# A read-back moved behind the attention projections, and adaLN weights loaded three steps ahead, in a two-layer diffusion step

## The chip, the cores and the metric

The kernel runs on one core of a Trainium2 chip. The core has five engines that run side by side, each with its own instruction stream: TensorE (PE, matrix products; its weight loads are shown as PEld), VectorE (DVE), ScalarE (ACT), GpSimd (POOL) and SyncE (SP), which here only issues DMA transfers. Sixteen DMA engines carry the transfers of the core. The metric is the device time of one launch in microseconds, the median over runs; smaller is better.

## What is computed

One inference step of a two-layer hybrid backbone over 128 context and 1024 latent tokens (a grid of 16 rows of 64), width 1024. Each layer is x + gate * mixer(rmsnorm(x) * (1 + scale) + shift), where shift, scale and gate come from a small adaLN product of the conditioning vector. Layer 0 mixes by a gated linear recurrence (4 heads, two directions) and a neighbourhood attention, layer 1 by a convolution and a second recurrence. The parts that matter here:

```python
def adaln(cond, w_mod, b_mod):
    m = (jax.nn.silu(cond) @ w_mod + b_mod)[:, None, :]
    return jnp.split(m, 3, axis=-1)

def even_mixer(h, w_in, w_out, lb, out_gain, rel_bias, s0, ctx_kv):
    q_a, z_f, z_b, v_a, g_a, q_b, k_b, v_b, g_b = jnp.split(h @ w_in, ...)
    o_a, s_fin = hgrn2_bidirectional(q_a, z_f, z_b, v_a, lb, s0)
    o_b = neighbourhood_attention(qh, kh, vh, ctx_kv[0], ctx_kv[1], rel_bias)
    y = concatenate([o_a * silu(g_a), o_b * silu(g_b)])
    return y @ w_out, s_fin, kh, vh

# in neighbourhood_attention: for each block of 16 columns a band of 32 key columns
    v_blk = lax.dynamic_slice_in_dim(v_grid, rs, kh, axis=2)[:, :, :, col_idx]
```

The attention gathers its values in column bands: four bands of 32 columns that start at 0, 8, 24 and 32.

## The kernel before

**Products and weights.** The tokens are cut into three chunks of 384. A projection's weights come in blocks of 512 KB (`wraw`), which ACT splits into a high part (`wh`) and POOL into the rest (`wl`, L186); each product is three matmuls of the parts (L316 to L318). A unit is one block of 128 features by one chunk: 24 matmuls of 128x384 (`unit_f`, L320), or 24 of 128x256 for the values (`unit_v`). Activations and splits by ACT are all recorded at L77.

**Order.** Every load (L56) and store (L59) goes through SP's one queue in the order of the program: a transfer that has to wait for its data or its buffer holds up all behind it. Twenty buffers of one shape ("slabs") are shared by weights raw and split (`wraw`, `wh`, `wl`), adaLN weights (`wm`), keys and queries (`kq`), value tiles (`vbt`) and value bands (`vband`). An agenda counts the units: `at(u, f)` puts a piece of work behind unit u, and `tick` (L350) runs what is due after each unit. There are eight semaphore lanes for DMAs, so a transfer also waits for the one eight before it.

**The stretch in question**, some 430 to 650 us into the span, follows the last head of the recurrence:
- 18 value units (`vb_unit`), in two blocks b of nine token tiles t. In the second, after every second tile, `band_copy` (L719) stores a finished `vbt` (512 KB, to the scratch tensor `vb_d`) and right behind it loads four pieces of 256 KB back into two `vband` tiles: the same values, cut to bands of 32 columns. These loads stand in SP's queue directly behind the store they read from. There are 4 stores and 16 such loads.
- 36 projection units (four feature blocks p; for each a key, a query and a gate weight, for each of these three chunks). `w_get(i, 0, 1)` loads the next weight one block ahead. Key and query units are evacuated into `kq` by ACT, gate units into `yT` by ACT and DVE (L365, `gate_evac`). Three PSUM buffers take turns.
- between the projection units the adaLN groups 1 and 2: 8 steps each, `mod_step(g, k)`, of 8 matmuls (L221) on two `wm` tiles of 512 KB; the step loads those of the next. After the eighth, a row is loaded (`bmrow`), DVE adds it (`modR`, L227), two `gate_d` stores put out the gates, and four transposes (L234) give the modulation. These stand in the same tick as the eighth step.

The attention itself, which reads `vband`, follows behind all 36 units.

Of the kernel before, what the change touches and what calls it, by code (L numbers as in the profile page):

```python
# [22 lines left out]
# columns of the packed small parameters (feature on the partition)  # L23
# [10 lines left out]
def trunk_kernel(ctx: ExitStack, tc: tile.TileContext, x, wm0, wm, bmr, wfe, wv, woe, wfo, woo, rgw, sm, st0,  # L34
# [34 lines left out]
    def act(out, in_, func, **kw):  # L69
        """An activation; those that need a table of their own stay between its load and the next one."""  # L70
# [12 lines left out]
    # ------------------------------------------------------------------ constants  # L83
# [39 lines left out]
    # decay floors: the first entry of the softmax over the two logits  # L123
# [12 lines left out]
    # log1p(exp(-|lam|)) + max(-lam, 0), as a series in z = e / (2 + e) <= 1/3  # L136
# [21 lines left out]
    # ------------------------------------------------------------------ weight stream  # L158
# [43 lines left out]
    # ------------------------------------------------------------------ adaLN rows  # L202
# [26 lines left out]

    def mod_feat(R, tag):  # L230
        """[128, j, g, 32] features on the partition, from row blocks at partitions 32 g."""
        pt = psum(tag)
        for j in range(4):
            PE.transpose(pt[:, j * 128:(j + 1) * 128], R[:, j * 128:(j + 1) * 128], ident)  # L234
        return pt.rearrange("p (j g c) -> p g j c", j=4, c=32)
# [14 lines left out]
    # ------------------------------------------------------------------ norm, modulation, split  # L250
    hT = {}

    def stats(xt, junk, cuts=(0, D)):
        """1 / sqrt(mean of squares + eps) of each row."""
# [34 lines left out]
    def to_hT2(l, c, ks, xn, tag):  # L289
        """Two blocks at once, each engine's steps together."""  # L290
# [18 lines left out]
    # ------------------------------------------------------------------ units of the projections  # L309
# [10 lines left out]
    def unit_f(i, c, tag=None):  # L320
        """Features of one block of 128 on the partition, one chunk of tokens."""
        ucount[0] += 1
        ps = psum(tag or ("o" if i >= IFO and ucount[0] % 4 == 0 else "mm"))
        o = ps[:, :CW]
        for k in range(8):
            mm_f(o, i, c, k)
        return o

    def unit_v(i, t):
        """Tokens on the partition, 256 features."""  # L330
# [29 lines left out]
    def gate_evac(key, o, twice=False):  # L360
        """o sigmoid(o); twice that by way of sigmoid(o) = (1 + tanh(o / 2)) / 2."""
# [22 lines left out]
    # ------------------------------------------------------------------ start  # L384
# [81 lines left out]
    # ------------------------------------------------------------------ layer 0, gated recurrence  # L466
# [17 lines left out]
    def ew1(h, d):  # L484
        """Log decays, their running sums in chunks of 64 and the sums' distances from each chunk's middle."""
# [61 lines left out]
    def att(h, d):  # L547
        """Scores in blocks of 64 keys and 64 queries; the two directions meet in the blocks on the diagonal."""
# [29 lines left out]
    def ew3(h, d):  # L578
        """The second chunk's queries as seen from the state before the tile; keys as the state after it sees them."""
# [18 lines left out]
    def kv(h, d, gi):  # L598
        """State before each latent tile; the state after the context."""
# [66 lines left out]
    # units from a head's projections to each of its steps  # L666
    STEP = [0, 1, 3, 4, 7, 9, 10, 11, 13, 15, 17, 20, 21, 21]

    def head(h, first=None):
# [16 lines left out]
        for n in range(4):          # q, z_f, z_b, g  # L686
# [15 lines left out]
    # ------------------------------------------------------------------ layer 0, attention projections  # L702
# [16 lines left out]
    def band_copy(Rg):  # L719
        src = vbt.pop(Rg)  # L720
        store(vb_d[2 * Rg:2 * Rg + 2].rearrange("t p f -> p t f"), src)
# [8 lines left out]
    for b in range(2):  # L730
        w_get(IVB + 2 * b + 1, 2, 1)
        for t in range(9):
            vb_unit(b, t)
            if t == 5:
                w_get(IVB + 2 * b + 1, 2, 2)
            if b == 1 and t in (2, 4, 6, 8):
                band_copy(t // 2 - 1)
# [4 lines left out]
    # adaLN, the other groups  # L742
    mst = {}

    def mod_step(g, k):
# [5 lines left out]
        if k < 7:  # L751
            mod_load(g, [k + 1])
        elif g == 1:
            mod_load(2, [0])
        if k == 7:
            R = mod_evac(g, mst["ps"], mod_row(g))
            if g == 1:
                gate_rows(0, R, 0)
                set_B(1, mod_feat(R, "b"), 2)
            else:  # L760
                set_A(1, mod_feat(R, "b"), 0)
                gate_rows(1, R, 2)
# [3 lines left out]
    def rows_of(c):  # L766
        """Grid rows of a chunk of tokens, cut at the middle row: (column in the chunk, first row, rows).
        A query tile holds its rows from the last to the first."""
# [138 lines left out]
    at(U + 2, mod_load, 1, [0])  # L907
    for g in (1, 2):
        for k in range(8):
            at(U + (4, 13)[g - 1] + k, mod_step, g, k)  # L910
    for p in range(4):
        for n in range(3):          # k, q, g
# [29 lines left out]
    # ------------------------------------------------------------------ layer 0, attention  # L942
# [15 lines left out]
    # ------------------------------------------------------------------ output projections  # L958
# [14 lines left out]
    def out_tiles(i0, ts, last=8, cuts=HALVES):  # L973
        """Row tiles of an output projection; the terms from last on come after those of all the tiles."""
# [14 lines left out]
    def resid(ps, gt, xt, cuts=HALVES):  # L989
        """xt += ps * gt; the product's tile is free afterwards."""  # L990
# [35 lines left out]
    # ------------------------------------------------------------------ layer 1  # L1026
# [13 lines left out]
    def xc_of(j, a, b):  # L1040
        """Tokens a to b of the convolution's result; the latents follow the context with a gap of 3."""
# [321 lines left out]
```

## Time and profile before

| | us |
|---|---|
| median of three runs | 1321.14 |
| the three runs | 1316.18, 1321.14, 1326.65 |
| span of the profiled execution | 1308.3 |
| PE busy | 1210.3 (93%) |
| PEld busy | 1076.2 (82%) |
| DVE busy | 692.2 (53%) |
| ACT busy | 540.4 (41%) |
| POOL busy | 380.4 (29%) |

The profiled execution's own time is not listed; only its span is. In the rows further down a timeline gives, for each group of equal instructions, the start, the duration, the engine and line, what it writes and reads, and in square brackets how long the engine was idle before it and what ended that wait. "SPq" is the queue of DMA issues on SP: its duration is the time until the last of them was issued, not until the data landed. [...]

### The profile page before, as it was taken

Reading aid. Unit: us, or ns where it says so; the run is one execution under the profiler, and the core shown is the slowest. Engines: PE = TensorE matmul, PEld = TensorE weight load, DVE = VectorE, ACT = ScalarE, POOL = GpSimd, SP = SyncE. Lnnn points to the kernel's source line nnn. Section 1 sums busy time; section 2 is a strip of 40 time slices with the busy share of each in tenths; the row PEclk is TensorE's granted clock in tenths of the full one; section 3 lists DMA queues with packets and bytes.
Section 4 is the critical chain, followed back from the end, with each engine's and each line's share of the span. In section 5 each row is a group of like instructions: output and inputs, shape, how many; then the busy total and the mean of one; then the engine's idle time right before and its main releaser. Section 6 shows DMA issues by size and latency. Waiting matters only on the chain.

```text
span 1308.3 us, 19176 instructions
## 1 busy us (share of the span) xinstructions
PE 1210.3 (93%) x7536; PEld 1076.2 (82%) x7536; DVE 692.2 (53%) x1422; ACT 540.4 (41%) x1065; POOL 380.4 (29%) x271
## 2 busy tenths in 40 slices
PE   4999999999999966999989999999989898988998
PEld 3889998999998964779966667888989798987886
DVE  5547128316365100000058897555568978799844
ACT  3435134334253201111136675323376676777311
POOL 0143023321414101111150420025445663645000
PEclk8999999999999997999979999999999989999999
DMA  9401000111101236562240215324001101112432
GB/s 353 179 33 37 17 19 23 53 33 37 33 23 43 95 120 208 173 209 75 65 158 13 95 66 177 113 81 145 17 25 41 41 25 41 41 33 81 145 129 81
DMA packets 41909, 110.45 MB, mean 84 GB/s; under 512 B 4180, under 2 KB 14804, under 8 KB 41820
## 3 DMA queue, kind: packets, MB, share of 16 engines
q1 hardware_dynamic: 41820, 109.24, 24.4%
q8 instruction: 59, 0.97, 0.3%
q14 instruction: 30, 0.25, 0.1%
HBM read 96.61 MB, written 12.61 MB: 83 GB/s over the span
## 4 chain that ended last, share of the span: by engine, by line
PE 36%; DVE 12%; ACT 6%; issue 4%; POOL 2%; DMA 1%; POOLq 0%; ACTq 0%; DVEq 0%; SPq 0%
PE ps_mm L316 5%; PE ps_mm L318 5%; PE ps_mm L317 5%; PE ps_mm L985 5%; PE ps_mm L984 4%; PE ps_mm L986 4%; DVE yT L1127 2%; DVE xc L1051 2%; DVE P L849 2%; ACT P L77 2%; ACT gr L77 1%; PE ps_a L221 1%; DMA bmrow<-in_bmr_dram 1%; DVE ps_mm L844 1%; ACT rt L77 1%
## 5 line engine op out<-in xcount | busy, mean ns | idle before, releaser
L316 PE MATMUL ps_mm<-hTh,wh 128*128 128x384 f32 x936 | 320.7, 347 | 9.9 <-ACT xp L77 4.8
L317 PE MATMUL ps_mm<-hTl,wh 128*128 128x384 f32 x936 | 319.8, 342 | 2.3 <-DVE hTl L307 1.7
L318 PE MATMUL ps_mm<-hTh,wl 128*128 128x384 f32 x936 | 319.4, 341 | 0.7 <-POOL wl L186 0.7
L186 POOL TENSOR_TENSOR wl<-wraw,wh 128x1024 fp32r<-128x1024 f32 x50 | 127.2, 2548 | 306.1 <-ACT wh L77 248.7
L316 PEld LDWEIGHTS ps_mm<-hTh,wh 128*128 128x128 f32 x936 | 177.8, 191 | 26.5 <-issue 6.5
L317 PEld LDWEIGHTS ps_mm<-hTl,wh 128*128 128x128 f32 x936 | 178.4, 191 | 4.8 <-DVE hTl L307 3.3
L318 PEld LDWEIGHTS ps_mm<-hTh,wl 128*128 128x128 f32 x936 | 178.2, 190 | 1.3 <-POOL wl L186 1.0
L985 PE MATMUL ps_mm<-wl,yh 128*128 128x512 f32 (+1 forms) x288 | 113.4, 394 | 4.6 <-DVE wl L186 4.5
L984 PE MATMUL ps_mm<-wh,yh 128*128 128x512 f32 (+1 forms) x288 | 112.7, 393 | 0.0
L986 PE MATMUL ps_mm<-wh,yl 128*128 128x512 f32 (+1 forms) x288 | 112.3, 390 | 0.0
L77 ACT ACTIVATE wh<-wraw 128x1024 fp32r<-128x1024 f32 x68 | 71.3, 1057 | 91.1 <-DMA wraw<-in_wfe_dram 67.3
L262 POOL TENSOR_TENSOR ss<-ss,nhalf 128x1 f32<-128x1 f32 x27 | 15.3, 565 | 242.9 <-DVE ss L261 185.8
L339 PE MATMUL ps_mm<-wh,hTh 128*128 128x256 f32 x288 | 82.6, 287 | 2.4 <-ACT va L77 2.4
L341 PE MATMUL ps_mm<-wh,hTl 128*128 128x256 f32 x288 | 81.2, 282 | 0.0
L340 PE MATMUL ps_mm<-wl,hTh 128*128 128x256 f32 x288 | 81.0, 281 | 0.0
L365 DVE SCALAR_TENSOR_TENSOR yT<-yT,ps_mm 128x384 f32<-128x384 f32 x10 | 5.5, 554 | 131.3 <-ACT yT L77 131.3
L77 ACT ACTIVATE res<-xt 128x512 f32<-128x512 f32 (+1 forms) x37 | 22.9, 619 | 123.3 <-DVE xt L994 115.5
L814 POOL TENSOR_TENSOR nbm<-mkt,bT 128x384 f32<-128x384 f32 x42 | 45.5, 1108 | 90.1 <-DVE nm L860 40.4
L985 PEld LDWEIGHTS ps_mm<-wl,yh 128*128 128x128 f32 x288 | 54.6, 189 | 19.0 <-DVE wl L186 7.7
L984 PEld LDWEIGHTS ps_mm<-wh,yh 128*128 128x128 f32 x288 | 54.5, 189 | 12.4 <-issue 0.3
L986 PEld LDWEIGHTS ps_mm<-wh,yl 128*128 128x128 f32 x288 | 54.4, 189 | 11.4
L1118 POOL TENSOR_TENSOR yT<-yT,rt 128x384 f32<-128x384 f32 x42 | 56.4, 1370 | 23.4 <-ACT rt L77 19.4
(260 smaller groups left out, 2477.3 us busy)
## 6 DMA issues: line engine op xcount, KB each, us to landing
wm<-in_wm_dram SPq DMA_DIRECT2D x48, 512.0 KB
wraw<-in_wfe_dram SPq DMA_DIRECT2D x28, 512.0 KB
xt<-in_x_dram SPq DMA_DIRECT2D x18, 512.0 KB
bT<-in_bias_dram SPq DMA_DIRECT2D x48, 192.0 KB
wraw<-in_wfo_dram SPq DMA_DIRECT2D x16, 512.0 KB
x_d<-xt SPq DMA_DIRECT2D x9, 512.0 KB
xt<-x_d SPq DMA_DIRECT2D x9, 512.0 KB
out_dram<-xt SPq DMA_DIRECT2D x18, 256.0 KB
```

The source lines that it names most:

```text
L77: i = A.activation(out, in_, func, **kw)
L186: (lo_eng or G).tensor_tensor(lo, r, hi.bitcast(F32), OP.subtract)
L316: PE.matmul(o, w1, hh, start=(k == 0), stop=False)
L317: PE.matmul(o, w1, hl, start=False, stop=False)
L318: PE.matmul(o, w2, hh, start=False, stop=(k == 7))
L339: PE.matmul(o, hh, w1, start=(k == 0), stop=False)
L340: PE.matmul(o, hh, w2, start=False, stop=False)
L341: PE.matmul(o, hl, w1, start=False, stop=(k == 7))
L984: PE.matmul(o[:, :q - p], yh[:, z], wh[:, p:q], start=(k == 0), stop=False)
L985: PE.matmul(o[:, :q - p], yh[:, z], wl[:, p:q], start=False, stop=False)
L986: PE.matmul(o[:, :q - p], yl[:, z], wh[:, p:q], start=False, stop=(k == 7))
L1118: G.tensor_tensor(us[c], us[c], r[:, c * CW:(c + 1) * CW], OP.mult)
```

## The change

Four things change, all in the stretch above; the computation is the same, and the rest of the diff takes comments out, which moves line numbers by up to nine.
- `band_copy` becomes `band_store`, in the same place, and `band_load`, put on the agenda at units U+20, U+23, U+26 and U+29 (U is the count at the start of the 36 projection units).
- The first three steps' `wm` loads (six of 512 KB) are issued in the second value block, ahead of tiles 2, 5 and 8.
- The 16 adaLN steps follow one another without a pause, at U+4 to U+19 (before: U+4 to U+11 and U+13 to U+20), and each loads the tiles of the step three further on.
- `mod_done` takes gate stores and transposes out of the eighth step to the next tick.

```diff
-    def band_copy(Rg):
-        src = vbt.pop(Rg)
-        store(vb_d[2 * Rg:2 * Rg + 2].rearrange("t p f -> p t f"), src)
+    def band_store(Rg):
+        store(vb_d[2 * Rg:2 * Rg + 2].rearrange("t p f -> p t f"), vbt.pop(Rg))
+
+    def band_load(Rg):
         v0 = vb_d[2 * Rg]
         for jp in range(2):
             t = slab("vband", (128, 2, 512))
...
         for t in range(9):
+            if b == 1 and t in (2, 5, 8):
+                mod_load(1, [t // 3])
             vb_unit(b, t)
             if t == 5:
                 w_get(IVB + 2 * b + 1, 2, 2)
             if b == 1 and t in (2, 4, 6, 8):
-                band_copy(t // 2 - 1)
+                band_store(t // 2 - 1)
...
-    def mod_step(g, k):
+    MODS = [(g, k) for g in (1, 2) for k in range(8)]
+
+    def mod_step(n):
+        g, k = MODS[n]
         if k == 0:
             mst["ps"] = psum("a")
         mod_mm(g, mst["ps"], [k])
         rows.pop((g, k, 0))
         rows.pop((g, k, 1))
-        if k < 7:
-            mod_load(g, [k + 1])
-        elif g == 1:
-            mod_load(2, [0])
+        if n + 3 < len(MODS):
+            mod_load(MODS[n + 3][0], [MODS[n + 3][1]])
         if k == 7:
-            R = mod_evac(g, mst["ps"], mod_row(g))
-            if g == 1:
-                gate_rows(0, R, 0)
-                set_B(1, mod_feat(R, "b"), 2)
-            else:
-                set_A(1, mod_feat(R, "b"), 0)
-                gate_rows(1, R, 2)
+            mst[g] = mod_evac(g, mst["ps"], mod_row(g))
+
+    def mod_done(g):
+        R = mst.pop(g)
+        if g == 1:
+            gate_rows(0, R, 0)
+            set_B(1, mod_feat(R, "b"), 2)
+        else:
+            set_A(1, mod_feat(R, "b"), 0)
+            gate_rows(1, R, 2)
...
     U = clock["u"]
-    at(U + 2, mod_load, 1, [0])
-    for g in (1, 2):
-        for k in range(8):
-            at(U + (4, 13)[g - 1] + k, mod_step, g, k)
+    for n in range(16):
+        at(U + 4 + n, mod_step, n)
+        if n % 8 == 7:
+            at(U + 4 + n + 1, mod_done, MODS[n][0])
+    for Rg in range(4):
+        at(U + 20 + 3 * Rg, band_load, Rg)
```

The order of SP's queue around the second value block was this; `fin` are final states and `vbc` the context's values, both stored to the output:

```order
L59 DMA out_dram<-vbc 128x512
L59 DMA out_dram<-fin 128x128 x2
L59 DMA vb_d<-vbt 128x2x512
L56 DMA vband<-vb_d 128x1x512 x4
L59 DMA vb_d<-vbt 128x2x512
L56 DMA vband<-vb_d 128x1x512 x4
L59 DMA vb_d<-vbt 128x2x512
L56 DMA vband<-vb_d 128x1x512 x4
L59 DMA vb_d<-vbt 128x2x512
L56 DMA vband<-vb_d 128x1x512 x4
L56 DMA wm<-in_wm_dram 128x1024 x2
L59 DMA out_dram<-kq 128x128
```

Of the change, the same place:

```order
L59 DMA out_dram<-vbc 128x512
L56 DMA wm<-in_wm_dram 128x1024 x2
L59 DMA out_dram<-fin 128x128 x2
L59 DMA vb_d<-vbt 128x2x512
L56 DMA wm<-in_wm_dram 128x1024 x2
L59 DMA vb_d<-vbt 128x2x512
L56 DMA wm<-in_wm_dram 128x1024
L59 DMA vb_d<-vbt 128x2x512
L56 DMA wm<-in_wm_dram 128x1024
L59 DMA vb_d<-vbt 128x2x512
L56 DMA wraw<-in_wfe_dram 128x1024
L59 DMA out_dram<-kq 128x128
```

The 16 reads of `vb_d` are gone from between the stores, and six `wm` loads stand there in their place, ahead of the projections.

On the same queue, the end of the projections, before, where the last `wm` loads and the last projection weights (`wraw`) are issued:

```order
L56 DMA wraw<-in_wfe_dram 128x1024
L56 DMA wm<-in_wm_dram 128x1024 x3
L59 DMA out_dram<-kq 128x128
L56 DMA wm<-in_wm_dram 128x1024
L56 DMA bmrow<-in_bmr_dram 128x1x512
L56 DMA wraw<-in_wfe_dram 128x1024
L59 DMA gate_d<-modR 2x512 x2
L56 DMA wraw<-in_wfe_dram 128x1024 x3
L59 DMA out_dram<-kq 128x128
```

And of the change:

```order
L59 DMA out_dram<-kq 128x128
L56 DMA vband<-vb_d 128x1x512
L59 DMA gate_d<-modR 2x512 x2
L56 DMA vband<-vb_d 128x1x512 x3
L56 DMA wraw<-in_wfe_dram 128x1024
L56 DMA vband<-vb_d 128x1x512 x4
L56 DMA wraw<-in_wfe_dram 128x1024
L56 DMA vband<-vb_d 128x1x512 x4
L56 DMA wraw<-in_wfe_dram 128x1024
L56 DMA vband<-vb_d 128x1x512 x4
L59 DMA out_dram<-kq 128x128
L56 DMA wraw<-in_wfe_dram 128x1024
```

The last four projection weights (those of gate block 2, key block 3, query block 3 and gate block 3) now each have reads of `vb_d` ahead of them, three or four at a time, and the second read stands behind the two `gate_d` stores.

On ACT, from the last evacuation of query block 2 on, before (a `yT` is an evacuation of a gate unit, a `kq` one of a key or query unit, a `wh` the split of a weight):

```order
L77 ACTIVATE kq<-ps_mm 128x6x4x16
L77 ACTIVATE wh<-wraw 128x1024
L77 ACTIVATE yT<-ps_mm 128x384 x3
L77 ACTIVATE kq<-ps_mm 128x384 x2
L77 ACTIVATE wh<-wraw 128x1024
L77 ACTIVATE kq<-ps_mm 128x384
```

And of the change:

```order
L77 ACTIVATE kq<-ps_mm 128x6x4x16
L77 ACTIVATE yT<-ps_mm 128x384
L77 ACTIVATE wh<-wraw 128x1024
L77 ACTIVATE yT<-ps_mm 128x384 x2
L77 ACTIVATE kq<-ps_mm 128x384 x2
L77 ACTIVATE wh<-wraw 128x1024
L77 ACTIVATE kq<-ps_mm 128x384
```

The split of the weight for query block 3 moved from ahead of the three `yT` to between the first and the second of them.

## Rows read from the trace of the kernel before

**Rows 1.** The page, first lines: span, and busy time of PE.
```profile
span 1308.3 us, 19176 instructions
...
PE 1210.3 (93%) x7536; PEld 1076.2 (82%) x7536; DVE 692.2 (53%) x1422; ACT 540.4 (41%) x1065; POOL 380.4 (29%) x271
```
**Rows 2.** Waits, 430 to 660 us: us in total, times, longest.
```profile
ACT wh L77 <- DMA wraw<-in_wfe_dram: 57.8, 7, 36.3
...
PE ps_a L221 <- DMA wm<-in_wm_dram: 20.3, 1, 20.3
...
POOL wl L186 <- DMA vb_d<-vbt: 8.6, 1, 8.6
...
PE ps_b L234 <- DVE modR L227: 2.3, 2, 1.8
```
**Rows 3.** PE's timeline, 453 to 516 us: start, duration.
```profile
455.45 0.46 PE L627 MATMUL ps_o<-va,at 128*128 128x128 f32 x2 [1.18 <-DVE on L638]
...
500.01 3.09 PE L221 MATMUL ps_a<-wm,condS 128*32 128x512 f32 x8 [20.26 <-DMA wm<-in_wm_dram]
504.40 0.69 PE L316 MATMUL ps_mm<-hTh,wh 128*128 128x384 f32 x1 [1.30 <-ACT kq L77]
...
510.45 1.07 PE L221 MATMUL ps_a<-wm,condS 128*32 128x512 f32 x8
...
515.85 1.06 PE L221 MATMUL ps_a<-wm,condS 128*32 128x512 f32 x8
```
**Rows 4.** SP's timeline of DMA issues, 436 to 495 us.
```profile
436.86 2.41 SPq L56 DMA_DIRECT2D vband<-vb_d  x4
439.75 1.61 SPq L59 DMA_DIRECT2D vb_d<-vbt  x1
451.38 2.42 SPq L56 DMA_DIRECT2D vband<-vb_d  x4
...
480.07 2.39 SPq L56 DMA_DIRECT2D vband<-vb_d  x4
482.56 2.46 SPq L56 DMA_DIRECT2D wm<-in_wm_dram  x2
...
494.54 0.33 SPq L56 DMA_DIRECT2D wm<-in_wm_dram  x1
```
**Rows 5.** Windows: stretch, length, busy of PE, PEld, DVE, ACT, POOL, clock, DMA share, GB/s.
```profile
446.00:450.00 4.00, 4.00 (x37) 4.00 (x37) 0.17 (x1) 1.27 (x7) 0.00 (x0) 1.00 0.28 104
474.00:478.00 4.00, 4.00 (x26) 3.96 (x26) 1.14 (x2) 0.00 (x0) 0.00 (x0) 1.00 0.26 96
```
**Rows 6.** Windows, the wait of PE: the clock stands third from the end.
```profile
490.00:500.00 10.00, 0.00 (x0) 0.02 (x1) 0.00 (x0) 0.00 (x0) 0.00 (x0) 0.50 0.92 229
```
**Rows 7.** The chain that ended last, in order of time: start, duration, what.
```profile
587.52 1.94 PE ps_a L221 x8
...
589.47 6.15 DMA bmrow<-in_bmr_dram
...
595.74 0.70 DVE modR L227
```
**Rows 8.** Timelines of ACT, POOL and DVE: a split, and evacuations of units.
```profile
502.91 1.06 ACT L77 ACTIVATE wh<-wraw 128x1024 fp32r<-128x1024 f32 x1 [36.27 <-DMA wraw<-in_wfe_dram]
625.88 0.49 ACT L77 ACTIVATE kq<-ps_mm 128x384 f32<-128x384 f32 x1 [3.72 <-PE ps_mm L318]
642.73 0.39 ACT L77 ACTIVATE kq<-ps_mm 128x256 f32<-128x256 f32 x1 [3.60 <-PE ps_mm L318]
621.59 2.39 POOL L186 TENSOR_TENSOR wl<-wraw,wh 128x1024 fp32r<-128x1024 f32 x1 [10.33 <-PE ps_mm L317]
622.19 0.55 DVE L365 SCALAR_TENSOR_TENSOR yT<-yT,ps_mm 128x384 f32<-128x384 f32 x1 [3.68 <-ACT yT L77]
```
**Rows 9.** PE's timeline, a wait elsewhere in the span.
```profile
979.81 0.69 PE L316 MATMUL ps_mm<-hTh,wh 128*128 128x384 f32 x1 [4.84 <-ACT xp L77]
```
**Rows 10.** Windows, the stretch around that wait.
```profile
979.00:986.00 7.00, 6.19 (x19) 6.19 (x20) 7.00 (x11) 3.88 (x9) 3.11 (x1) 0.51 0.01 2
```
**Rows 11.** Waits of SP's queue, 390 to 670 us.
```profile
SPq L56 <- PE ps_mm L318: 52.1, 12, 18.4
```

## The prediction

> **What bounds the kernel now.** I read the page first: one core, and PE is busy for 93% of the span [rows 1]. What a change can give here is therefore what PE waits, or runs at half clock. Next I read the waits of all engines from 430 to 660 us, the stretch in which the value bands, the two adaLN groups and the attention projections lie, and for each PE wait the row of PE's timeline behind it.
>
> The largest is 20.26 us: the first adaLN step starts at 500.01 and waited for its `wm` tiles [rows 2, 3]. SP's timeline says why. The fourth read-back of a value band is issued at 480.07, and only behind it, at 482.56, the `wm` loads [rows 4]. SP got there late because each read-back waits in the queue for the store ahead of it to land: the store issued at 439.75 released its band reads at 451.38, 11.6 us later [rows 4]. And the reads are slow: in two stretches in which little else is in flight the DMA share is 0.26 to 0.28 at 96 to 104 GB/s [rows 5], so they run on about four engines of 16.
>
> [...] ACT, meanwhile, waited 36.3 us for a weight that is queued behind the same loads [rows 2], and five evacuations stood behind it: PE loses another 1.30 at 504.40.
>
> **What the change removes.** The gain is a sum over PE's waits in this stretch:
> - 1.2: at 455.45 PE waits for DVE on L638 [rows 3]. The root is POOL's split, which waited 8.6 for a store `vb_d<-vbt` [rows 2] to free its slab; without reads between the stores that store lands at once.
> - 20.3: the hole itself. The first `wm` loads now stand ahead of the first `vb_d` store, more than 40 us before their use.
> - 2.0: the step at half clock, 3.09 less 1.07 [rows 3].
> - 1.3 and 1.7: the wait at 504.40, and the unit behind it, partly at half clock: 510.45 less 504.40 is 6.05, against 4.33 for a unit between two steps (515.85 less 510.45 less 1.07) [rows 3].
> - 2.3: PE's two waits for `modR` at L234 [rows 2]. The transposes now come one tick later, behind a whole unit of 4.2, and the row that `modR` adds is loaded at the same place, so some 4 us more cover a wait of at most 1.8.
> - 0.9: the last adaLN step takes 1.94 where 1.06 is usual, waiting for its tiles [rows 7, 3]; three steps of lead cover that.
>
> Sum 29.7. With nothing on the other side the time is 1321.14 - 29.7 = 1291.4. The profiled execution's own time is not listed; its span is 12.8 below the median of the three runs, and I take the differences as they are onto that median.
>
> The 16 adaLN steps cost the same 16 times 1.06, the projections the same 36 units, and no transfer is added or dropped. Three steps of lead hold six slabs of `wm` where two were held, while the eight `vband` slabs are free until step 20: that comes out even, and no wait is charged.
>
> **What the moved reads cost.** The 16 reads now stand in SP's queue between the weights of the last projections. Where they start: the first waits for nothing, but the second stands behind the two `gate_d` stores, which wait for `modR` of group 2. The last step was at 587.52; it is now 28.3 earlier (the sum without its own 0.9 and the last 0.5 of the transposes) and a unit of 4.2 earlier still ((642.73 - 625.88) / 4 [rows 8]), as the pause between the groups is gone: 555.0. From there to the end of `modR` took 8.9 with a step that was 0.9 too long [rows 7], so 8.0: reads go out from 563.0 on.
>
> How fast: 100 GB/s, the middle of 104 and 96. For start and landing I add 2.7: the four reads before 451.38 and a quarter of the store that is spread over all engines, 1.18 MB, took from 436.9 to 451.4 or 14.5 us (the four were issued just before the store of 439.75 [rows 4]), and 11.8 of that is the stream. The queue on these four engines then holds three reads (0.79 MB), a quarter of the weight for the third gate block (0.13 MB), four reads, a quarter of the weight for the fourth k block, four reads, a quarter of the weight for the fourth q block: 3.28 MB or 32.8 us. That last weight lands at 563.0 + 2.7 + 32.8 = 598.5. Every weight has three quarters on free engines, but is complete only with the last quarter.
>
> Who waits: in ACT's order the split of this weight now stands between the first and second evacuation of gate block 2 (units 24 to 26). Unit 28 takes the PSUM buffer of unit 25, so it needs that split (1.06), ACT's 0.49 and DVE's 0.55 [rows 8]: 600.6. It would start at 625.88 - 29.7 = 596.2: 4.4 late. The last four reads wait for a slab that POOL's split of the same weight frees (598.5 + 1.06 + 2.39 = 602.0), and the last weight behind them lands 2.7 + 11.8 later, at 616.5; with its split and the evacuation behind it 618.0. Unit 32 would start at 642.73 - 29.7 = 613.0 [rows 8]: 5.0 late, with the 4.4 in it. As a formula, with k = 100 GB/s over the rate, the delay is the larger of 32.8 k - 28.4 and 44.6 k - 39.6.
>
> A wait of 5.0 can bring the clock down: after an idle 4.84 a stretch ran at 0.51 [rows 9, 10]. I charge 1.7, what the unit at 504.40 lost; it is 0 if the wait falls into two short ones. Net: 29.7 - 5.0 - 1.7 = 23.0, so 1321.1 - 23.0 = **1298**.
>
> **Bounds of the rate.** From above: at 115 GB/s both delays are gone by the formula, and a faster read gives nothing more. From below: of the four reads issued from 480.07 on, the third had landed when SP issued at 494.54 [rows 4], with weights in flight on the same engines; 0.79 MB in 14.5 is 54 GB/s, and 67 with the 2.7 taken off. I take the value of the clean stretches, since after the change one weight per 12.6 us shares the engines, not two `wm` tiles at once.
>
> [...]
>
> **The rivals.**
> - A, the reads are hidden: 1291. For it: 104 GB/s needs only a little more, and the reads could go out earlier if `modR` does. Against it: no row shows four engines above 104.
> - B, the reads run at about 80 GB/s, as those of the 14.5 us with start and landing counted in: delay 16.2, with 1.7 of clock 1309.
> - C, on the other side: sharing with weights takes the reads to 60 GB/s, between the 54 and 67 at 494.54. Delay 34.7 and 1.7 are 6.7 more than the gain: 1328 (1336 at 54). The place is PE before units 24 to 33, waiting on ACT behind a late split; it decides below 66 GB/s.
> - D, the lead isn't there: SP is one queue, and a wait for a slab held by the projections stopped it for 18.4 at the longest [rows 11]. Three steps are 16.2 ahead; with 6.2 to land (as `bmrow` [rows 7]) a step would be 8.4 late; with the 5.0 and 1.7 the time is 1306. Against it: 18.4 occurred once, the mean of these waits is 4.3.
>
> **How the numbers follow.** Forecast 0.42 (1295 to 1303), A 0.28, B 0.15, D 0.07, C 0.08. The time is the forecast's. The range from 1287 to 1309 has A with some spread of the measurement below (the runs lie within 5 us of their median), the forecast, D, and the better half of B: about 0.84. A difference under 1% (13 us) can't be told from none: below 1308 are A, the forecast, most of D and a third of B, 0.81; above 1334 only the worst of C, 0.03; the rest 0.16.
>
> **What would show it.** In the trace after: no PE wait over 2 us from 450 to 530 and adaLN steps of 1.07 from the first; SP's `gate_d` near 563 and the reads behind it; DMA share near 0.3 at about 100 GB/s behind that; a PE wait of some 4 us near 596 or 613 whose releaser is ACT, and ACT's own wait for a `wraw` there. No such wait means A; waits of over 10, B or C. Wrong altogether if PE still waits for `wm`, or if the kernel after the projections changes: from the attention on, no engine's order is altered.

## The result, and the profile after

The changed kernel takes 1299.68 us (median of 4 runs) beside 1322.85 us of the kernel before (4 runs); the ratio is 0.987, 95% interval 0.983 to 0.9915. (The medians by themselves give 0.982, just outside this interval: one of the four runs of the changed kernel took 1316.6, which the median leaves aside; the means give 0.986.) Measured again beside other kernels it was 0.986 (0.980 to 0.992). The spans of the two traces, 1308.3 and 1297.5, lie only 10.8 apart: the recurrence ahead of the stretch, whose instructions are the same, ran at half clock for some time in the second trace (from 400 to 420 the granted clock, which the profile gives as a share of TensorE's full speed, is 0.66 there and 1.00 before) and in those below, which are 4 to 28 us late by then.

So the traces are compared inside the stretch. PE has the same 7536 matmuls in the same or nearly the same order; the table takes the start of the 3000th (last head of the recurrence), the 3750th (near unit 24 of the projections), the 4000th (near unit 33) and the 4250th (first part of the attention).

| start of PE's matmul, us | 3000th | 3750th | 4000th | 4250th |
|---|---|---|---|---|
| before | 448.8 | 602.8 | 646.7 | 694.7 |
| after | 457.6 | 580.7 | 635.9 | 683.7 |
| after less before | +8.9 | -22.1 | -10.8 | -10.9 |

Up to the 3750th the change wins 31.0 us, from there to the 4000th it gives back 11.3, and from there to the end the difference stays as it is: -10.9 at the 4250th, -10.8 at the last.

The first part. PE's timeline of after, near the first adaLN steps, which answers to [rows 3]:

```profile
487.13 1.07 PE L221 MATMUL ps_a<-wm,condS 128*32 128x512 f32 x8
...
492.53 1.07 PE L221 MATMUL ps_a<-wm,condS 128*32 128x512 f32 x8
```

No wait stands in brackets: the 20.26 us for `wm` are gone, and the first step takes 1.07 where it took 3.09, behind a wait with a granted clock of 0.50 [rows 6]. SP's timeline of DMA issues answers to [rows 4]:

```profile
432.28 2.16 SPq L56 DMA_DIRECT2D wm<-in_wm_dram  x2
...
463.58 0.38 SPq L59 DMA_DIRECT2D vb_d<-vbt  x1
464.05 0.42 SPq L56 DMA_DIRECT2D wraw<-in_wfe_dram  x1
...
570.27 0.57 SPq L59 DMA_DIRECT2D gate_d<-modR  x2
570.89 1.72 SPq L56 DMA_DIRECT2D vband<-vb_d  x3
572.71 0.90 SPq L56 DMA_DIRECT2D wraw<-in_wfe_dram  x1
573.70 9.23 SPq L56 DMA_DIRECT2D vband<-vb_d  x4
583.02 0.90 SPq L56 DMA_DIRECT2D wraw<-in_wfe_dram  x1
584.02 11.37 SPq L56 DMA_DIRECT2D vband<-vb_d  x4
595.48 2.39 SPq L56 DMA_DIRECT2D wraw<-in_wfe_dram  x1
612.30 2.68 SPq L56 DMA_DIRECT2D vband<-vb_d  x4
```

The first `wm` loads leave 55 us ahead of their use. Further down the reader sees the reads of the bands between the last weights. Four issues take 9 to 11 us there, where the three at 570.89 take 1.72. It is not the lanes that hold them: the lane of the issue that lasts from 576.92 to 580.14 had been free since 571.5. An issue takes 2.5 to 3.2 us, which is about the pace at which the reads land; why SP is held to it is not shown.

The second part. Rows of PE's timeline of after with their waits:

```profile
597.70 0.44 PE L316 MATMUL ps_mm<-hTh,wh 128*128 128x384 f32 x1 [1.79 <-ACT kq L77]
...
610.80 0.44 PE L316 MATMUL ps_mm<-hTh,wh 128*128 128x384 f32 x1 [2.92 <-DVE yT L365]
...
630.30 0.69 PE L316 MATMUL ps_mm<-hTh,wh 128*128 128x384 f32 x1 [2.58 <-ACT kq L77]
```

And ACT's rows at the same three places:

```profile
596.22 1.06 ACT L77 ACTIVATE wh<-wraw 128x1024 fp32r<-128x1024 f32 x1 [10.34 <-issue]
597.18 0.47 ACT L77 ACTIVATE kq<-ps_mm 128x384 f32<-128x384 f32 x1
597.55 0.48 ACT L77 ACTIVATE yT<-ps_mm 128x384 f32<-128x384 f32 x1
608.73 1.06 ACT L77 ACTIVATE wh<-wraw 128x1024 fp32r<-128x1024 f32 x1 [10.70 <-DMA wraw<-in_wfe_dram]
609.69 0.85 ACT L77 ACTIVATE yT<-ps_mm 128x384 f32<-128x384 f32 x2
...
628.82 1.06 ACT L77 ACTIVATE wh<-wraw 128x1024 fp32r<-128x1024 f32 x1 [13.05 <-DMA wraw<-in_wfe_dram]
629.78 0.47 ACT L77 ACTIVATE kq<-ps_mm 128x384 f32<-128x384 f32 x1
```

Three times ACT stands 10 to 13 us at a split whose weight has not landed, and the evacuations behind it, which PE waits for, had been ready. The first of these rows names no weight ("issue"), but its landing can be told from the marks of landing, of which the trace has sixteen for each weight. Of this one, issued at 583.02, twelve marks lie at 587.15 to 587.56 and the last four at 595.65 to 596.14, just ahead of the split at 596.22. The two other weights look alike: twelve marks by 601.88 and 622.07, the last at 608.65 and 628.73. So three quarters of each weight were there some 7 to 9 us ahead of the quarter that shares its engines with the reads.

The windows of after (columns as in [rows 5]) give the rate of the reads and the clock behind the first and the third wait:

```profile
588.00:592.00 4.00, 4.00 (x25) 4.00 (x24) 0.00 (x0) 0.00 (x0) 0.00 (x0) 1.00 0.26 102
598.00:602.00 4.00, 4.00 (x17) 4.00 (x16) 0.55 (x1) 0.03 (x1) 1.79 (x1) 0.63 0.66 177
630.00:634.00 4.00, 3.70 (x14) 3.70 (x15) 0.00 (x0) 1.25 (x5) 2.38 (x1) 0.60 0.00 0
```

The reads run at 102 GB/s with a DMA share of 0.26. The clock dips to 0.63 behind the first wait and to 0.60 behind the last. The three waits are 7.3 us, a wait of 0.48 for POOL's split comes on top, and the remaining 3.5 of the 11.3 are what those dips cost (1.5 and 1.6 by the two windows), with small gaps.

### The profile page after: what moved, and what is told of

Read it like the earlier page. It is cut to its first block, busy times and chain, and to the rows that moved or that the text cites. A ratio compares the mean times of both kernels' runs of the same rounds, so it can differ in the third digit from the quotient of the medians.

```text
span 1297.5 us, 19173 instructions
## 1 busy us (share of the span) xinstructions
PE 1218.8 (94%) x7536; PEld 1085.6 (84%) x7536; DVE 692.1 (53%) x1422; ACT 539.2 (42%) x1065; POOL 380.4 (29%) x271
## 4 chain that ended last, share of the span: by engine, by line
PE 55%; DVE 13%; ACT 6%; issue 4%; DMA 3%; POOL 2%; SPq 1%; POOLq 0%; ACTq 0%; DVEq 0%
PE ps_mm L316 8%; PE ps_mm L318 7%; PE ps_mm L317 7%; PE ps_mm L994 5%; PE ps_mm L995 5%; PE ps_mm L993 5%; DMA wraw<-in_wfe_dram 3%; DVE yT L1136 2%; DVE P L856 2%; DVE xc L1060 2%; ACT P L77 1%; PE ps_mm L339 1%; PE ps_mm L341 1%; PE ps_mm L340 1%; PE ps_a L221 1%
```

## The experiments

For each kernel the ratio to the kernel before, and what its trace gained or lost between the same matmuls, in us less the trace before: A from the 3000th to the 3750th (the hole and the adaLN steps), B from there to the 4000th (the last projections), C from there to the 4250th (the start of the attention).

| kernel | ratio (95%) | A | B | C |
|---|---|---|---|---|
| after, first measurement | 0.987 (0.983 to 0.9915) | -31.0 | +11.3 | -0.1 |
| after, again | 0.986 (0.980 to 0.992) | -31.0 | +9.9 | +0.9 |
| E1, lead only | 1.010 (1.006 to 1.0135) | +7.5 | -0.3 | +0.4 |
| E2, reads moved only | 0.987 (0.980 to 0.9935) | -30.6 | +16.6 | -4.3 |
| E3, after with wide reads | 0.972 (0.964 to 0.9805) | -31.0 | -0.5 | +1.6 |
| E4, after with 64 reads | 0.983 (0.977 to 0.989) | -31.0 | +5.8 | +2.4 |
| E5, after, weights earlier | 0.985 (0.980 to 0.989) | -30.8 | +7.7 | +1.8 |
| E6, after, dimension 2 by 2 | 0.982 (0.978 to 0.986) | -31.0 | +9.8 | +1.2 |
| E7, before with wide reads | 0.972 (0.967 to 0.977) | -27.5 | 0.0 | -4.2 |
| E8, before with 32 reads | 0.987 (0.979 to 0.995) | -19.0 | +0.2 | +3.0 |
| E9, after with 32 reads | 0.985 (0.979 to 0.9905) | -31.0 | +6.7 | +2.5 |
| E10, lead and 32 reads | 0.983 (0.977 to 0.989) | -22.0 | -0.2 | +1.0 |
| E11, E9 one unit later | 0.983 (0.977 to 0.989) | -30.9 | +0.5 | +8.2 |

**After, again.** No edit.

> The changed kernel again, beside the others on one chip. Theory: as in the first measurement, ratio to before 0.987 (0.982 to 0.992). In its trace, whatever the clock does upstream, the part from the first adaLN step to the first attention matmul shows the same three waits of PE, before units 25 to 33 of the projections, of 2 to 3 us each, with ACT or DVE as releaser, and no wait for wm. Rival (the waits are an accident of one execution): other places or none.

Waits of 1.92 and 4.49 at the first two places and none for `wm`, but no third over 0.45 and one of twice the size: the places hold for two of the three waits, the sizes vary. B is 9.9 where it was 11.3.

**E1 and E2, the two halves of the change.** E1 keeps the three steps of lead and puts the reads back behind their stores:

```diff
                 band_store(t // 2 - 1)
+                band_load(t // 2 - 1)
...
-    for Rg in range(4):
-        at(U + 20 + 3 * Rg, band_load, Rg)
```

> Only the adaLN part of the change: weights three steps ahead, gate stores and transposes one tick later; the reads of the value bands stay behind their stores, as before. Theory (the four-engine reads delay everything behind them in the queue): the wait for wm goes, but the weight of gate block 0, issued behind the last four reads near 482, lands only near 495, so PE waits some 11 us for it or for ACT behind its split; of the 25 us of the hole and its clock some 12 are gained, with 3 more at the group ends: 15 us, ratio 0.989 (0.984 to 0.994). No wait before units 24 to 33. Rival (the one step of lead is the cause of the hole): all of the 31 us that the changed kernel gained before its late waits, ratio 0.977.

Both missed: the lead alone makes the kernel slower, by 1%. A row of PE's timeline of E1, one of ACT's, and rows of SP's:

```profile
522.42 0.69 PE L316 MATMUL ps_mm<-hTh,wh 128*128 128x384 f32 x1 [27.24 <-ACT kq L77]
```

```profile
518.26 1.06 ACT L77 ACTIVATE wh<-wraw 128x1024 fp32r<-128x1024 f32 x1 [38.27 <-DMA wraw<-in_wfe_dram]
```

```profile
464.58 1.95 SPq L59 DMA_DIRECT2D vb_d<-vbt  x1
476.72 1.40 SPq L56 DMA_DIRECT2D wm<-in_wm_dram  x2
478.21 3.65 SPq L56 DMA_DIRECT2D vband<-vb_d  x4
481.96 3.04 SPq L56 DMA_DIRECT2D wm<-in_wm_dram  x2
485.09 0.55 SPq L59 DMA_DIRECT2D vb_d<-vbt  x1
498.93 2.60 SPq L56 DMA_DIRECT2D vband<-vb_d  x4
501.62 2.05 SPq L59 DMA_DIRECT2D out_dram<-kq  x1
503.71 0.57 SPq L56 DMA_DIRECT2D wraw<-in_wfe_dram  x1
```

PE does not wait for `wm` any more, but 27.24 us for ACT, which stands at the split of the next weight (38.3 us of wait for `wraw`). That weight is issued at 503.71, behind the fourth group of reads, and these behind a store that needed 13.8 us to land, from 485.09 to 498.93 (before, the fourth store took 11.8): the `wm` loads that were put among the reads lengthen what each store waits for. My sum for E1 took the last reads at the time of before, and missed that. (A second explanation, that the larger number of slabs in use made this hole, is tried in E10.) The waits for `modR` did not go with the lead either; they are 3.04 and 2.14 in E1.

E2 is the other half:

```diff
-            if b == 1 and t in (2, 5, 8):
-                mod_load(1, [t // 3])
...
-        if n + 3 < len(MODS):
-            mod_load(MODS[n + 3][0], [MODS[n + 3][1]])
+        if n + 1 < len(MODS):
+            mod_load(MODS[n + 1][0], [MODS[n + 1][1]])
...
+    at(U + 2, mod_load, 1, [0])
     for n in range(16):
-        at(U + 4 + n, mod_step, n)
+        at(U + 4 + n + n // 8, mod_step, n)
         if n % 8 == 7:
-            at(U + 4 + n + 1, mod_done, MODS[n][0])
+            at(U + 4 + n + n // 8, mod_done, MODS[n][0])
```

> Only the read-back moved; adaLN as before, one step ahead, a tick's pause between the groups, gate stores in the eighth step. Theory: the hole goes, since nothing but the four stores stands ahead of the first wm loads (they are issued near 465 and used near 480): 27 us, the waits for modR and the last step stay. The reads start some 6 us later than in the changed kernel (the pause and the waits that stay), so the late waits grow from 11 to about 16: net 11 us, ratio 0.991 (0.985 to 0.997). Rival (lead is the cause): a hole of 10 us or more for wm at the first adaLN step, ratio 1.0 or above.

With the reads gone from there one step of lead is enough: A is -30.6, as good as in the whole change. The waits for `modR` and the late last step, which were expected to stay, are gone as well. The late waits are longer, as the theory had it. Two rows of PE's timeline of E2:

```profile
592.97 0.69 PE L316 MATMUL ps_mm<-hTh,wh 128*128 128x384 f32 x1 [3.12 <-ACT kq L77]
...
637.38 0.69 PE L316 MATMUL ps_mm<-hTh,wh 128*128 128x384 f32 x1 [6.15 <-ACT kq L77]
```

Its `gate_d` stores go out at 577.55, that is 566.0 less the 11.6 that its 3000th matmul was late; in after it is 570.27 less 8.9 or 561.4. So the reads start 4.6 later, and the weight of key block 3 lands 5.1 later: at 604.01 less 11.6, beside 596.14 less 8.9 in after. B is 5.3 larger. That the delay follows the start one for one is not shown by this alone, for in E2 the built order of ACT differs too: the splits for key block 3 and query block 3 stand one evacuation later than in after. The lead and the group change are worth about 5 us in B, and not more in A than 0.4. In the time the two can't be told apart.

**E3 and E7, what the slow reads cost.** E3 is the changed kernel, E7 the kernel before, each with this edit, which reads as many bytes at the same place, but other rows:

```diff
-                                          ap=[[64 * 512, 4], [512, 32], [1, 512]]))
+                                          ap=[[512, 128], [1, 512]]))
```

> The changed kernel, with each of the 16 reads taking 128 rows of the scratch that lie one behind the other instead of 4 times 32: the same bytes at the same place of the queue, with an outermost dimension of 128 in place of 4 (the attention then gets other values than the reference's). Theory (the late waits come from four slow engines): the DMA share in the reads goes from 0.26 to near 1 and the rate above 200 GB/s; the three late waits vanish, and with them 11 us: ratio 0.977 (0.972 to 0.982). Rival (the waits come from the place in the queue, the slab or the two stores ahead, not from the rate): the same waits as in the changed kernel, ratio 0.987.

> The kernel before, reads in their old place behind each store, but of 128 rows one behind the other (outermost dimension 128, same bytes; the attention gets other values than the reference's). Theory (the hole at the first adaLN step is made by four slow engines, not by the place): a store is no longer held up behind reads and lands within 3 us, so the last reads are issued near 460 and the wm loads behind them land well before 480: no hole, 26 us gained; the two waits for modR and the late last step stay: ratio 0.980 (0.974 to 0.986). Rival (it is the place: SP waits for each store to land, whatever the rate): a hole of 10 us or more stays, ratio 0.993 or above.

Both came out for the theory, and faster than it said: E3 at the lower end of its range, E7 beyond it (0.972 where 0.974 was the least). In E3 PE has no wait over 0.45 between the first adaLN step and the attention, and windows during its reads show 16 engines at work:

```profile
572.00:576.00 4.00, 4.00 (x27) 3.96 (x26) 0.24 (x2) 0.49 (x1) 0.00 (x0) 1.00 0.79 231
576.00:580.00 4.00, 4.00 (x25) 4.00 (x24) 0.00 (x0) 1.17 (x3) 0.00 (x0) 1.00 1.01 372
580.00:584.00 4.00, 4.00 (x25) 4.00 (x24) 0.00 (x0) 0.87 (x5) 2.41 (x1) 1.00 1.09 400
```

372 to 400 GB/s stand in place of 102, at the same place of the queue and in the same order of ACT as in after (from the 3000th to the 4100th matmul its instructions follow one another alike in both traces). E7 says more: with fast reads there is no hole at the first adaLN step even where the reads stand behind their stores. PE's timeline of E7:

```profile
484.31 1.07 PE L221 MATMUL ps_a<-wm,condS 128*32 128x512 f32 x8
...
525.61 0.66 PE L234 MATMUL ps_b<-cs,modR 128*128 128x128 f32 x4 [1.42 <-DVE modR L227]
```

A is -27.5, where 26 us were expected; what is missing to -31.0 are the wait for `modR` in the second row and late steps. Another 4.2 come in C, which was in no expectation and has to do with the clock (see E11). Both the hole of before and the late waits of after are thus made by the same thing, 4 MB of reads at 100 GB/s; the change moves them to a place where they cost 11 us in place of 25. Neither kernel is of use as it is, since the attention gets other rows; the two only price the reads.

**E4, E6 and E5, the reads and their place.** E4 cuts each read into four of 32 rows (`ap=[[512, 32], [1, 512]]`, one for each grid row), with the bands as they were.

> The changed kernel with each read of 4 times 32 rows cut into four reads of 32 rows (64 KB, outermost dimension 32), so 64 reads in place of 16 at the same places; the values are the same. Theory: each read now runs on 16 engines; SP needs about 0.56 us to issue one, so a group of 16 takes 9 us of SP in place of the 10.5 us of four slow reads, and weights are no longer queued behind them on four engines: the weight of query block 3 lands near 594 in place of 598.5 (times of the trace before, shifted), early enough; late waits at most 2 us, ratio 0.977 (0.972 to 0.984). Rival (small reads cost SP or the DMA engines more than they save): the weights are issued later, waits of 5 us or more as in the changed kernel, ratio 0.987 or above.

B falls to 5.8, less of a gain than the theory had, though no wait is over 2 us, as it said. The reads ran at 137 GB/s with a share of 0.53 (576 to 580), where after has 102 and 0.26. The rows of PE's timeline say what is left:

```profile
605.39 0.45 PE L316 MATMUL ps_mm<-hTh,wh 128*128 128x384 f32 x1 [1.53 <-ACT wh L77]
...
607.88 0.56 PE L318 MATMUL ps_mm<-hTh,wl 128*128 128x384 f32 x1 [1.69 <-POOL wl L186]
```

and ACT's rows of E4:

```profile
603.90 0.49 ACT L77 ACTIVATE yT<-ps_mm 128x384 f32<-128x384 f32 x1 [3.72 <-PE ps_mm L318]
604.29 2.00 ACT L77 ACTIVATE wh<-wraw 128x1024 fp32r<-128x1024 f32 x2
```

Neither weight is late here: ACT splits two at once without a wait for them. They stand in its order behind the last evacuation of gate block 2, where in after they stood ahead of it, so PE has reached the units that need them. The order of ACT is made when the kernel is built, and the shape of the reads changed it.

E6 writes the same read as 2 times 2 grid rows (`ap=[[128 * 512, 2], [64 * 512, 2], [512, 32], [1, 512]]`).

> The changed kernel with the outermost dimension of each read cut from 4 to 2 times 2 rows, same values. Theory: the engines of a transfer are counted from that dimension, so two engines of 16 carry it: DMA share 0.13 and about 50 GB/s; the formula of the prediction (44.6 k - 39.6 with k = 2) gives a delay of 50 us where the changed kernel has 5: some 45 us slower than it, ratio to before 1.02 (1.00 to 1.04). Rival (the number of engines hangs on the partitions of the tile, or the dimensions are merged on the way): the same share of 0.26 and the same time, ratio 0.987.

The rival holds. A window of E6:

```profile
588.00:592.00 4.00, 4.00 (x25) 4.00 (x24) 0.00 (x0) 0.00 (x0) 0.00 (x0) 1.00 0.26 102
```

That is the share and the rate of after, and B is 9.8. The marks of landing agree with about four engines: each read has one early mark and four late ones, in E6 as in after (there, of the read issued at 564.10, one at 565.07 and four from 569.22 to 569.42). The theory of this run was a conjecture and did not come: the share was to be 0.13 and is 0.26. The two outer dimensions together have the strides of one of 4; why the share stayed is not shown. The run leaves the formula of the prediction untested at half the rate.

E5 loads the last weights two blocks ahead:

```diff
-            w_get(i, 0, 1 if i + 1 < IWE else 0)
+            w_get(i, 0, min(IWE - 1 - i, 2 if i >= IP + 5 else 1))
```

> The changed kernel, with the weights of the last projection blocks loaded two blocks ahead in place of one, from query block 1 on: in SP's queue each late weight stands one group of four reads earlier, the reads are as slow as before. Theory: the weight of query block 3 lands near 587 (needed at 596), that of gate block 3 near 599 (needed at 613): no late waits though the DMA share stays at 0.26 in the reads, ratio 0.977 (0.972 to 0.982). Rival (slabs: the second weight in flight waits for one, and stops the queue): waits as before or longer, ratio 0.987 or above.

The theory fell. The last of the three waits is gone, the others are 3.28 and 2.53, and B is 7.7. The weights do land when the theory said: less the 17.4 that the trace is late, the splits for query block 3 and gate block 3 start at 588.2 and 600.4, as their weights land (587 and 599 expected). But ACT's order as built has their splits a block earlier too, again ahead of evacuations. ACT's rows of E5:

```profile
605.65 1.06 ACT L77 ACTIVATE wh<-wraw 128x1024 fp32r<-128x1024 f32 x1 [10.96 <-DMA wraw<-in_wfe_dram]
606.62 0.47 ACT L77 ACTIVATE kq<-ps_mm 128x384 f32<-128x384 f32 x1
...
617.80 1.06 ACT L77 ACTIVATE wh<-wraw 128x1024 fp32r<-128x1024 f32 x1 [10.33 <-DMA wraw<-in_wfe_dram]
618.77 0.85 ACT L77 ACTIVATE yT<-ps_mm 128x384 f32<-128x384 f32 x2
```

What hurts here is not that a weight comes later than its unit, but that its split stands in a queue ahead of work that PE waits for.

**E8 to E11, fast reads that keep the bands.** Both bands of a tile start 8 columns apart, so that one read can take 32 rows by 2 bands (32 reads in all):

```diff
-            for jj in range(2):
-                load(t[:, jj, :], bass.AP(tensor=v0.tensor, offset=v0.offset + BS[2 * jp + jj] * 512,
-                                          ap=[[64 * 512, 4], [512, 32], [1, 512]]))
+            for r in range(4):
+                load(t[32 * r:32 * r + 32], bass.AP(tensor=v0.tensor, offset=v0.offset + (64 * r + BS[2 * jp]) * 512,
+                                                    ap=[[512, 32], [8 * 512, 2], [1, 512]]))
```

E8 has it in the kernel before, E9 in the changed one, E10 in E1; E11 is E9 with `band_load` at U+21, U+24, U+27 and U+30.

> The kernel before with its reads in their old place and with the same values, each cut along the four grid rows and joined over the two bands of a tile (32 rows by 2 by 512, 128 KB, outermost dimension 32): 32 reads in place of 16. Theory (only the four slow engines made the hole): SP issues a group of eight in some 4.5 us, the stores land in about 3, so the first wm loads are issued near 471 and land before 480: no hole, 26 us gained as with the reads of 128 rows: ratio 0.973 (0.967 to 0.980). Rival (twice the issues hold up SP's queue): wm is issued behind 480, a hole of 5 us or more, ratio 0.985 or above.

> The changed kernel with the same 32 faster reads, in the new place. Theory: no wait for a transfer is left before units 24 to 33, but ACT's order, which is fixed when the kernel is built, has the splits for key block 3 and query block 3 one behind the other after the last evacuation of gate block 2, as in the kernel with 64 reads; PE waits some 3 us there and runs some 3 to 4 us at half clock: ratio 0.981 (0.975 to 0.987). Rival (the waits of the kernel with 64 reads came from its many issues): half as many issues, no wait, ratio 0.973.

> The 32 faster reads in the old place behind each store, together with the adaLN weights three steps ahead. Theory: with fast reads the lead no longer digs its hole of 27 us (it came from reads, stores and wm loads behind one another on slow engines); the waits for modR and the late step go as well, 2 to 3 us more than without the lead: ratio 0.971 (0.964 to 0.978). Rival (the hole of the lead alone comes from slabs, 6 for wm and 8 for the bands at once): PE waits 5 us or more for the weight of gate block 0, ratio 0.985 or above.

> The changed kernel with the 32 faster reads, put one unit later (U+21, U+24, U+27, U+30). In the order as built each of the last weights now stands ahead of its reads in SP's queue, ACT has the split for key block 3 ahead of the evacuations of gate block 2 and that for query block 3 behind them, and every adaLN step is one piece on PE. Theory (two causes together: slow reads, and ACT's fixed order): no wait of PE over 1 us between the first adaLN step and the attention, all of the 31 us: ratio 0.974 (0.968 to 0.980), better than the changed kernel. Rival (the reads hold up the queue whatever their order): waits of 3 us or more before units 27 to 33, ratio 0.982 or above.

E8 missed in the time: 0.987, beyond its range. What it said of the hole came true. The first `wm` loads leave at 469.02 and there is none; the window from 466 to 470, in which the last group of reads runs, shows a DMA share of 0.92 and 238 GB/s. At the 3250th matmul the kernel is 25.0 ahead (493.4 against 514.7, with 3.7 late at the 3000th). But 6.0 of it are lost by the 3750th. PE's timeline of E8:

```profile
490.22 1.05 PE L221 MATMUL ps_a<-wm,condS 128*32 128x512 f32 x4
...
492.10 1.05 PE L221 MATMUL ps_a<-wm,condS 128*32 128x512 f32 x4
```

A step of eight matmuls in one piece takes 1.07, as shown above for after; in two pieces each half takes 1.05. The order as built cuts six of the 16 steps in two, some 1.0 each (one of them ahead of the 3250th matmul), and one wait for `modR` of 2.20 stays, behind which the clock falls (0.57 from 580 to 584).

E9 is as expected: the same waits of 1.53 and 1.69 at the splits as in E4, in the same order of ACT, and B 6.7. Half as many issues change nothing, so the number of issues was not the cause.

E10 missed in the time as well: 0.983, beyond its range, with A at -22.0. No wait of PE over 0.45 is left but those for `modR`, 2.83 at 554.46 and 2.06 at 598.69, which the theory had gone; behind both the clock falls (0.63 from 556 to 560, 0.58 from 600 to 604). The chain of E10 shows the cause of the first: `bmrow`, the row that DVE adds to make `modR`, was issued at 544.32, behind three `wm` loads, and took 9.27 to land. The hole of 27 us that the lead dug in E1 is gone with the fast reads, so slabs did not make it.

E11 missed in the time too: 0.983, beyond its range. What it said of the waits came true: B is +0.5 and PE has no wait over 0.3 before the attention: both causes of the late waits, slow reads and ACT's order, are out, and nothing else is left of them. The time is that of after, within the intervals: 8.2 us are lost at the start of the attention. Windows of E11, and then of after, at that place:

```profile
656.00:660.00 4.00, 4.00 (x16) 2.24 (x16) 2.19 (x7) 1.32 (x4) 3.27 (x4) 0.50 0.53 190
...
672.00:676.00 4.00, 4.00 (x14) 2.37 (x13) 0.83 (x5) 0.60 (x1) 0.00 (x0) 0.50 0.33 93
```

```profile
656.00:660.00 4.00, 4.00 (x12) 2.04 (x11) 3.54 (x13) 2.38 (x7) 3.01 (x3) 0.50 0.53 197
...
668.00:672.00 4.00, 4.00 (x35) 2.69 (x36) 3.41 (x9) 1.86 (x4) 3.09 (x4) 1.00 0.20 70
```

By the windows PE is at a granted clock of 0.50 from about 648 to 679 in E11, some 31 us, and from about 654 to 667 in after, some 14. Half of the difference, the work lost at half clock, is 8.5, near the 8.3 between their columns C. At the other end, E7 has 1.00 in all windows from 640 to 680, and E2 from 650 to 680; their C is -4.2 and -4.3. So column C is for the most part this. Whether the longer stretch of E11 comes from its own order or would be another in the next execution was not tried, so whether it beats the changed kernel stays open.

## Why the prediction was right

It said 1298, in 1287 to 1309; measured were 1299.7. Point by point:

**The gain of the first part.** 26.5 of the 29.7 were to come from the hole and what hangs on it; between the 3000th matmul and the 3225th (510.5 before, 492.5 after) the change wins 26.8. For `modR` and the last step 3.2 were charged; up to the 3750th another 4.2 come. By the starts of the matmuls, which are the same in number on every line there, 2.6 of these are the waits at the transposes and 1.0 late steps; the rest are gaps of under 0.3 us. No PE wait at L234 and none for `wm` is left in after. The sum is 31.0 against 29.7. What the prediction had wrong here is the credit: it gave the lead in loading its part, and E2 shows that the moved reads alone bring -30.6.

**The start, the rate, the landing.** Less the 8.9 that the trace is late: `gate_d` at 561.4 (predicted 563.0), 102 GB/s at a share of 0.26 (100, about four engines), the split of the weight for query block 3 at 599.9 (landing 598.5), the last reads issued at 603.4 (602.0), the last split at 620.0 (landing 616.5). E3 confirms that the rate is the cause; E2 agrees with a delay that follows the start, as far as its other order of ACT lets it.

**Who waits.** Right on the engine and on the mechanism, ACT's queue. The term was too small: 5.0 and 1.7 for the clock, against 11.3. What it had wrong is the last weight. Its split was to start at 616.5 and started 3.5 later: the weight before it was 1.4 late, and from the issue of the last reads to the split went 16.5 where 2.7 and 11.8 were charged. (The marks of landing show the four reads complete at 617.96, 621.63, 624.68 and 627.35, that is 3.7, 3.1 and 2.7 apart where 2.6 is the pace of 100 GB/s, and then a small store and the weight at 628.73.) Since the units also came 1.3 earlier than thought, the delay at that place is 5.0 + 3.5 + 1.3 = 9.8, which holds the earlier waits and their clock; the 1.5 that are left of 11.3 fit the dip to 0.60 from 630 to 634 (4 times 0.4 is 1.6). So the clock fell twice, behind waits of 1.79 and 2.58, where one fall was charged and nothing for short waits. I also left out the split for key block 3, which stands ahead of an evacuation too: by the prediction's terms it lands at 563.0 + 2.7 + 21.0 = 586.7 and makes unit 26 (due at 587.8) 0.4 late; it was 1.79. That wait is part of the 9.8, since of delays on one path the last decides.

**The engines of the reads.** The prediction took about four engines from a share of 0.26 to 0.28, and that this holds in the new place was its estimate. After has 0.26 there, at 102 GB/s, and the time followed the 102. E3, with reads of 128 rows, has 1.01 and 1.09, E6 0.26. What sets the number of engines is not shown.

**The net.** In the stretch it is 31.0 - 11.3 = 19.7, less than the predicted 23.0. The medians differ by 23.2, but the ratio's interval reaches from 11 to 22 us of 1322. That the time came within 2 us of the forecast is thus in part luck: its parts were off by 1.3 and 4.6, and the four runs of the changed kernel lie between 1299 and 1317.

**The rivals.** A, hidden reads, did not come; E3 shows what it would have given. In size D (8.4, 5.0 and 1.7, or 15.1) and B (16.2 and 1.7, or 17.9) lay nearer to the 11.3 than A or C, but neither came by its mechanism: for B the rate was 102 and not 80, and for D no step was late, though SP's queue did wait up to 17.4 us for the projections' matmuls, as in [rows 11]. C did not come.

## What to carry to other kernels

Before a slow transfer is moved, look at its DMA share and ask why it is slow: here the same bytes on all engines, left where they were (E7) or moved (E3), were worth some 30 us in the stretch, and moving them at their old pace 20. Those fast reads took rows that were not the bands. The kernels that read the bands at a higher share (E4 with 0.53, E8 with 0.92, E9 to E11 with the reads of E8) lost part of this to other causes, an order of ACT or PE made at the build, late `bmrow` and the clock, and none of them is shown to beat the change: their ratios are 0.983 to 0.987. When loads move, read on the engine behind them (here ACT) where the work that waits for them stands in the built order, since it holds up all that is behind it: in after three splits held ACT for 10 to 13 us each. Loading further ahead did not help here where the earlier loads joined a queue that was already the bound: E1 lost 1% with it.

## What the runs showed of the hardware

- Reads of 4 times 32 rows, 256 KB, ran at 102 GB/s with a DMA share of 0.26 (after, 588 to 592); reads of 128 rows, 256 KB, at 372 to 400 GB/s with a share of 1.0 and more (E3, 576 to 584).
- A weight of 512 KB that was queued behind reads on four engines had twelve of its sixteen marks of landing 4.5 us after its issue and the last one 13.1 us after it (after, issue at 583.02); its split on ACT began 0.1 us behind the last.
- The adaLN step on PE takes 1.07 us for eight matmuls in one piece (after), and 1.05 for four (E8): two pieces cost twice as much.
- TensorE's granted clock was 0.63 and 0.60 in the stretches behind waits of 1.79 and 2.58 us in after, shorter ones than that of [rows 9]; behind the wait of 2.92 between them it was 1.00 (610 to 618).
